# Decoder layer on one core: values' differences in the attention, a later statistic of the recurrence, and three moved pieces of VectorE work

## The chip, the cores and the metric

The kernel runs on one core of one Trainium2 chip. The core has five engines, each of which executes its own list of instructions in order: TensorE (PE in the profile, with its weight loads as PEld), VectorE (DVE), ScalarE (ACT), GpSimd (POOL) and SyncE (SP, which here only issues transfers). They meet through semaphores. The metric is the time of one execution on the device, in microseconds (us); lower is better.

## The reference

One decoder layer over x of shape (1, 512, 1024): a SwiGLU feed-forward half step, a mixer, and a second feed-forward half step, each with an RMS norm ahead of it and one behind it, before the residual is added.

```python
for l in range(DEPTH):                                    # DEPTH = 1
    x = x + 0.5 * rms_norm(swiglu(rms_norm(x, ffn1_pre_g[l]), ffn1_w_gu[l], ffn1_w_down[l]), ffn1_post_g[l])
    y = hybrid_mixer(rms_norm(x, mix_pre_g[l]), ...)
    x = x + rms_norm(y, mix_post_g[l])
    x = x + 0.5 * rms_norm(swiglu(rms_norm(x, ffn2_pre_g[l]), ffn2_w_gu[l], ffn2_w_down[l]), ffn2_post_g[l])
```

The mixer projects its input, runs a gated recurrence (RG-LRU) on 512 channels and attention on the other 512, and projects both back:

```python
y_lru  = rg_lru(x_lru, conv_w, conv_b, w_rg, b_rg, w_ig, b_ig, lam) * gelu(gate_lru)
y_attn = sliding_window_sink_attention(q, k, v, sinks)
y = concatenate([rms_norm(y_lru, g_lru_out), rms_norm(y_attn, g_attn_out)]) @ w_o
```

In the recurrence log_a = 8 · r · log_sigmoid(lam), where lam is a parameter of 512 numbers; its log_sigmoid does not depend on x. The attention has 8 query heads, 2 key/value heads of 64, blocks of 128 queries and a window of 128 keys. A query i of block b sees the keys j ≤ i of its own block and the keys j > i of the block before it, 128 keys in all, and a sink that enters the denominator only:

```python
rel = qi + BLOCK_Q - kj                  # kj runs over the block before and the block itself
band = (rel >= 0) & (rel < WINDOW)
p = exp(scores - m);  denom = sum(p) + exp(sink - m)
out = (p / denom) @ v_band
```

The FFN width is 2816. All inputs are float32.

## The kernel before

**Arithmetic.** Activations are kept transposed: 128 features on the partitions, 512 tokens along the row. A float32 product on TensorE is made of three fast ones: each operand is split into a rounded high part (a cast on ScalarE, tiles `whi_…`, `hha`, `hhs`, `xch`) and the rest (a subtraction, mostly on VectorE, tiles `wlo_…`, `hla`, `hls`, `xcl`), and high·high, high·low and low·high are added up in PSUM (`mm3`, lines 511 to 513). The FFN products use seven products of half-size blocks for eight, so VectorE also makes sums and differences of weight blocks (line 296, 329) and of activations (lines 868 and 880, tiles `s3a`, `s4a`).

**Order.** The kernel writes each engine's order out by hand: instructions stand on each engine in the order in which the program issues them, and nothing is reordered. A class of weight units (`W`) works ahead of TensorE: `W.fill(n)` casts and subtracts units until n more are ready than have been taken, `W.take()` hands one over (and fills ahead itself). There are six pairs of high and low tiles. A unit comes out of one of the raw tiles that SP loads; when the last unit of a raw tile is split, SP issues the load of the next one.

**FFN1** runs over five groups of its width. A group's gate and up products are made by `octo`, which takes pieces of other work to issue beside its products (`beside`, by the product they go with); from the third group on, these are the forms of the group before, for `seven_down`, the down products. In group g = 2 one more piece goes there, `decay_factor` (line 1290): log_sigmoid(lam) and its multiples, 17 small VectorE operations on 128x4 numbers, and one Exp on ScalarE, which needs another activation table than the Silu around it.

**The end of a sublayer** (`boundary`, and the last LATE of the 8 chunks of 128 features): the down products of these chunks are made half of the tokens at a time; VectorE adds each to its partial sum (line 697, `yp_a<-ay`), ScalarE squares it, VectorE adds the square to the sum (lines 710 and 714), TensorE sums over the features (`InvRms.stats`, line 555), ScalarE and VectorE form 1/rms as a diagonal matrix `dg`, and TensorE spreads it over the partitions (`InvRms.spread`, line 569). The loop over the late chunks takes each chunk's weights and calls `W.fill(3)`.

**The mixer.** `in_parts` (line 1548) takes a projection's PSUM bank, scales it by the inverse norm `R` (`scaled`, line 1489, tiles `kT` and `qT`), copies its first 128 columns aside (line 1551, into `home`) and splits the rest. Attention runs in 8 units (block b, key/value head n) with four heads each. For a unit, `scores` makes q·k, the exponentials follow, `turn_p` transposes them to `pt`, ScalarE copies them to `pa`, and GpSimd's `affine_select` sets the masked part to zero. For the first block only the own block's keys count. For b > 0 the rows of the block before and those of the own block share one set of 128 columns, since a query sees complementary parts of them: `pp` keeps the part for the block before and `pa` that for the own. `values` multiplies them with `v`, whose 65th column per head is one, so that the denominator falls out with the output. `v`, the first queries and keys all lie in the tile `home[0]`.

**The output projection of the mixer** (lines 1873 to 1908): five early chunks (EARLY) of 128 output features, four feature blocks `ysp[4..7]` of the attention and four, `ysp[0..3]`, of the recurrence. `wo_attn` makes the attention's part first; meanwhile the recurrence's norm (`lrms`, two halves) is finished: its sum of squares `acc_lru` is added up on VectorE, then come `stats`, `dg_lru`, `spread`, and per block two VectorE multiplications (line 1898), a cast on ScalarE (`ylh`) and a subtraction on VectorE (`yll`). Then the products of `ysp[0]` to `ysp[3]` follow.

Of the kernel before, what the change touches and what calls it, by code (L numbers as in the profile page):

```python
# [15 lines left out]
P = 128  # L16
T = 512
# [105 lines left out]
def tile_layer(ctx: ExitStack, tc: tile.TileContext, out: bass.AP, **ins: bass.AP):  # L123
# [1312 lines left out]
    for g, (f0, f1) in enumerate(GROUPS1):  # L1436
        if g:
            beside = hid.seven_forms_of(before, h_hbm[before], dealt_halves=True) if g > 1 else {}
# [109 lines left out]
    def in_parts(b, first, name, low=dve):  # L1548

        x = scaled(wt(name), b)  # L1550
        dve.tensor_copy(first, x[:, :P])
# [159 lines left out]
    def turn_p(b, n):  # L1711
# [7 lines left out]
        pp = None  # L1719
        if b > 0:  # L1720
            pp = wt(f"pp{b}{n}")
            pool.affine_select(v4(pp), v4(pa), pattern=[[0, NB], [-1, P]], base=0, channel_multiplier=1, compare_op=ALU.is_gt, fill=0.0)
        pool.affine_select(v4(pa), v4(pa), pattern=[[0, NB], [1, P]], base=0, channel_multiplier=-1, compare_op=ALU.is_ge, fill=0.0)
        unit[b, n] = pa, pp

    def values(b, n):
        pc, pp = unit[b, n]
# [5 lines left out]

        for j in range(4):
# [138 lines left out]
    def wo_attn(cs):  # L1873
        ks = range(KC, KD)
        for k in ks:
            for c in cs:
                for part in ws[c]:
                    pe.matmul(banks[c], part[:, k, :], ysp[k][0], start=k == KC and part is ws[c][0], stop=False)
        for c in cs:
            for k in ks:  # L1880
                pe.matmul(banks[c], ws[c][0][:, k, :], ysp[k][1], start=False, stop=False)

    ws, banks = [], []
    for c in range(EARLY):
# [4 lines left out]
        wo_attn(range(c + 1) if c == EARLY - 3 else [c])  # L1889
        if c == EARLY - 3:  # L1890
            for l in lrms:
                l.stats()
            W.fill(3)
        if c == EARLY - 2:
            bcs = [l.spread() for l in lrms]
            for ci in range(KC):
                for h in range(2):
                    dve.tensor_mul(hl[ci][:, HALF[h]], hl[ci][:, HALF[h]], bcs[h])
                y = t2k(f"ylh{ci}", F32R), t2k(f"yll{ci}", F32R)
                x_high(y, hl[ci], col("g_lru_out", ci), ALL)  # L1900
                x_low(y, hl[ci], col("g_lru_out", ci), ALL)
                ysp[ci] = y
# [205 lines left out]
```

## Time and profile before

| | |
|---|---|
| three runs | 840.01, 841.22, 841.30 us (median 841.22) |
| the profiled execution | 840.68 us, its span in the profile 838.7 us |
| TensorE busy | 830.4 us (99% of the span) |
| VectorE busy | 732.4 us (87%) |
| ScalarE busy | 519.2 us (62%) |
| GpSimd busy | 166.8 us (20%) |
| granted TensorE clock | 0.999 |
| DMA | 144.22 MB, mean 172 GB/s |

A row of a timeline gives the start in us from the span's start, the duration in us, the engine, the line of the kernel, the operation, the tile written and those read, the tile's shape, a count, and in brackets how long the engine was idle ahead of it and what ended that. "x2" or "x4" at a row's end means so many like instructions in a row, and the duration is of all. TensorE pipelines its products: the row of a 128x512 product says 0.39 us, but the next one of the same kind starts 0.23 us later. TensorE counts as busy while a product that has started waits within its row, so short waits do not show as idle time; they show when the distance from one start to the next is longer than for the same products elsewhere. The profiled execution takes 1.98 us more than its span.

### The profile page before, as it was taken

The page shows a single profiled execution, that of the slowest core. Times are in us where ns is not written, and L with a number is a line of the kernel's source. Part 1 is how long each engine was busy: PE and PEld are TensorE (multiplying, and loading weights), DVE is VectorE, ACT ScalarE, POOL GpSimd, SP SyncE. Part 2 cuts the span into 40 slices and gives each one's busy share as a digit, 9 for nine tenths or more (in the row PEclk, how much of TensorE's full clock was granted, in tenths as well). Part 3 has the DMA queues.
Part 4 walks back from the last instruction along what each step waited for, and adds up shares of the span by engine and source line. Part 5 has one row for each costly group of instructions (what it writes and reads, how often), then busy time and mean ns, then how long its engine had stood idle before and what let it go on. Part 6 is the DMA issues. An engine that isn't in the chain of part 4 may idle for free.

```text
span 838.7 us, 11907 instructions
## 1 busy us (share of the span) xinstructions
PE 830.4 (99%) x4252; PEld 705.9 (84%) x4252; DVE 732.4 (87%) x1036; ACT 519.2 (62%) x813; POOL 166.8 (20%) x188
## 2 busy tenths in 40 slices
PE   9999999999999999999999999999999999999997
PEld 9988888788888898987788899888888888888885
DVE  4989698999989978889789589997999799898996
ACT  6646556586666654556797446545758667676562
POOL 2022000041320325414531052002004023032001
PEclk9999999999999999999999999999999999999999
DMA  7276407299595797522511131667339939769742
GB/s 252 102 274 227 150 11 263 100 254 301 118 259 188 181 283 228 188 82 88 158 51 51 51 114 39 127 173 252 104 116 243 314 84 255 239 153 260 299 142 101
DMA packets 121851, 144.22 MB, mean 172 GB/s; under 512 B 24184, under 2 KB 76736, under 8 KB 121280
## 3 DMA queue, kind: packets, MB, share of 16 engines
q1 hardware_dynamic: 107824, 112.91, 42.1%
q0 software_dynamic: 13824, 30.42, 16.5%
q8 instruction: 33, 0.54, 0.2%
q14 instruction: 26, 0.21, 0.1%
q10 hardware_dynamic: 144, 0.13, 0.0%
HBM read 100.45 MB, written 39.32 MB: 167 GB/s over the span
## 4 chain that ended last, share of the span: by engine, by line
PE 89%; DVE 6%; DMA 2%; ACT 1%; issue 1%; DVEq 0%; POOL 0%; ACTq 0%; POOLq 0%
PE ab L968 10%; PE aa L968 9%; PE db L968 5%; PE da L968 5%; PE bb L968 3%; PE ba L968 3%; PE ya L1362 3%; PE yaa L1362 2%; PE yda L1362 2%; PE a_first L1230 1%; PE yab L1949 1%; PE yab L1948 1%; PE yab L1947 1%; PE yea L1362 1%; PE mn L529 1%; PE an L529 1%
## 5 line engine op out<-in xcount | busy, mean ns | idle before, releaser
L1140 POOL DMA_DIRECT2D yr_a<-stage x36 | 31.6, 1014 | 177.9 <-ACT stage L1137 157.1
L1140 POOL DMA_DIRECT2D yp_b<-stage x42 | 36.5, 1062 | 147.1 <-ACT stage L1137 117.9
L1963 POOL DMA_DIRECT2D yp_b<-stage x8 | 4.4, 547 | 65.2 <-ACT stage L1962 64.8
L691 POOL TENSOR_TENSOR acca_r<-acca_r,sq_r 128x512 f32<-128x512 f32 x6 | 9.0, 1505 | 40.0 <-ACT sq_r L541 39.9
L529 PE MATMUL an<-xh_mx,whi_xl 128*128 128x256 f32 x64 | 15.9, 288 | 0.0
L530 PE MATMUL an<-xh_mx,wlo_xl 128*128 128x256 f32 x64 | 15.5, 283 | 0.0
L2066 POOL TENSOR_TENSOR last<-yp,grow 128x512 f32<-128x512 f32 x3 | 3.9, 1300 | 56.1 <-DVE yp L2056 56.1
L2063 ACT ACTIVATE ysq<-yp 128x512 f32<-128x512 f32 (+1 forms) x8 | 4.9, 607 | 16.2 <-DVE yp L2056 16.2
L511 PE MATMUL gt<-xh_mx,whi_gt 128*128 128x512 f32 x32 | 14.3, 446 | 0.0
L1399 POOL DMA_DIRECT2D yp_a<-zy x16 | 8.8, 555 | 25.4 <-DMA rows_a<-yr_a 17.2
L511 PE MATMUL pq<-xh_mx,whi_q 128*128 128x512 f32 x32 | 12.8, 400 | 0.0
L511 PE MATMUL pub<-xh_f,whi_bu 128*128 128x512 f32 x32 | 12.7, 395 | 0.0
L513 PE MATMUL gt<-xh_mx,wlo_gt 128*128 128x512 f32 x32 | 12.6, 394 | 0.0
L511 PE MATMUL pgb<-xh_f,whi_bg 128*128 128x512 f32 x32 | 12.6, 393 | 0.0
L512 PE MATMUL gt<-xl_mx,whi_gt 128*128 128x512 f32 x32 | 12.5, 392 | 0.0
L512 PE MATMUL pq<-xl_mx,whi_q 128*128 128x512 f32 x32 | 12.5, 391 | 0.0
L513 PE MATMUL pq<-xh_mx,wlo_q 128*128 128x512 f32 x32 | 12.5, 390 | 0.0
L513 PE MATMUL pgb<-xh_f,wlo_bg 128*128 128x512 f32 x32 | 12.5, 390 | 0.0
L513 PE MATMUL pub<-xh_f,wlo_bu 128*128 128x512 f32 x32 | 12.5, 389 | 0.0
L512 PE MATMUL pgb<-xl_f,whi_bg 128*128 128x512 f32 x32 | 12.5, 389 | 0.0
L512 PE MATMUL pub<-xl_f,whi_bu 128*128 128x512 f32 x32 | 12.5, 389 | 0.0
L1362 PE MATMUL ya<-whi_ad,hha 128*128 128x512 f32 x32 | 12.4, 389 | 0.0
(2018 smaller groups left out, 3415.9 us busy)
## 6 DMA issues: line engine op xcount, KB each, us to landing
yp_b<-stage POOLq DMA_DIRECT2D x50, 256.0 KB, 8.9
yr_a<-stage POOLq DMA_DIRECT2D x44, 256.0 KB, 9.7
h_a<-za SPq DMA_DIRECT2D x16, 256.0 KB
h_b<-zb SPq DMA_DIRECT2D x16, 256.0 KB
hxb<-h_b SPq DMA_DIRECT2D x16, 256.0 KB
hxa<-h_a SPq DMA_DIRECT2D x6, 512.0 KB
xn<-in_x SPq DMA_DIRECT2D x8, 256.0 KB
raw_ad<-in_ffn_w_down SPq DMA_DIRECT2D x2, 1024.0 KB
```

What stands on the lines that cost most here:

```text
L511: pe.matmul(ps, hi[:, k, :], xh, start=start, stop=False)
L512: pe.matmul(ps, hi[:, k, :], xl, start=False, stop=False)
L513: pe.matmul(ps, lo[:, k, :], xh, start=False, stop=stop)
L529: pe.matmul(ps[:, sl], hi[:, k, :], xh, start=k == 0 and not goes_on, stop=False, skip_group_check=True)
L530: pe.matmul(ps[:, sl], lo[:, k, :], xh, start=False, stop=False, skip_group_check=True)
L691: eng.tensor_add(acc, acc, square(part, ALL, f"{self.name}{c}"))
L968: pe.matmul(b[tb], x[:, blk], w[:, k, :], start=first and q + k + j == 0, stop=q + k == 2 and j == 2, skip_group_check=True)
L1140: pool.dma_start(o, st, accum_op=ALU.add)
L1230: pe.matmul(banks[j][:, HALF[0]], ws[j][part][:, k, :], n1.xs[k][xpart][:, HALF[0]], start=k == 0 and part == xpart, stop=stop and k == KD ...
L1362: pe.matmul(o, x[:, blk], a[:, k, :], start=start and j == 0, stop=stop and j == 2, skip_group_check=True)
L1399: (pool if q % 2 else sync).dma_start(chunks[32 * q:32 * (q + 1), :, i * P:(i + 1) * P], turned[32 * i:32 * (i + 1), :, q])
L1947: pe.matmul(banks[i], hh[:, js], hi[:, k, :], start=first and k == 0, stop=False, skip_group_check=True)
```

## The change

It has five parts.

1. `decay_factor` is issued beside the third product of group g = 1 instead of group g = 2.
2. In the loop over FFN1's late chunks `W.fill(3)` becomes `W.fill(2)`.
3. `in_parts` makes the first 128 columns by a multiplication from the PSUM bank, ahead of `scaled`, instead of a copy behind it.
4. The attention's values: for b > 0 the unmasked weights `pa` are multiplied with the block before, and the masked ones (`pc`, the own block's part) with the difference of the two blocks' values. The second `affine_select` of these six units goes. The differences are made by two subtractions, one of 128x325 ahead of the last query chunk's `lru_gates`, and one of 128x65 in the third turn of the attention loop, into the place of the keys that have been used by then.
5. The recurrence's norm: `stats` moves from ahead of the fourth early chunk to the middle of its attention part, `spread` and the four blocks' work from ahead of the fifth chunk to its fourth product, and `W.fill(3)` ahead of them becomes `W.fill(2)` there and `W.fill(1)` behind the loop.

```diff
             beside = hid.seven_forms_of(before, h_hbm[before], dealt_halves=True) if g > 1 else {}
-            if g == 2:
-                beside[2] = [lambda: decay.append(decay_factor())]
...
+            beside = hid.seven_forms_of(before, h_hbm[before], dealt_halves=True) if g > 1 else {2: [lambda: decay.append(decay_factor())]}
...
                 late.append((c, W.take(0)))
-                W.fill(3)
+                W.fill(2)
...
     def in_parts(b, first, name, low=dve):
+        dve.tensor_mul(first, b[:, :P], R[:, :P])
         x = scaled(wt(name), b)
-        dve.tensor_copy(first, x[:, :P])
...
         b = in_product(f"pq{j}")
+        if j == KC - 1:
+            e = HD + 1
+            steps_of_v = [k0[:, :e]] + [home[0][:, P + 2 * T + i * e:P + 2 * T + (i + 1) * e] for i in range(8, 13)]
+            dve.tensor_sub(home[0][:, P + 2 * T + 8 * e:P + 2 * T + 13 * e], v[:, 3 * e:], v[:, e:6 * e])
...
-        pp = None
-        if b > 0:
-            pp = wt(f"pp{b}{n}")
-            pool.affine_select(v4(pp), v4(pa), ..., compare_op=ALU.is_gt, fill=0.0)
-        pool.affine_select(v4(pa), v4(pa), ..., compare_op=ALU.is_ge, fill=0.0)
-        unit[b, n] = pa, pp
+        pc = wt(f"pc{b}{n}") if b > 0 else pa
+        pool.affine_select(v4(pc), v4(pa), ..., compare_op=ALU.is_ge, fill=0.0)
+        unit[b, n] = pa, pc
...
             if b > 0:
-                pe.matmul(o, pp[:, hs], rows(b - 1), start=True, stop=False)
-            pe.matmul(o, pc[:, hs], rows(b), start=b == 0, stop=True)
+                pe.matmul(o, pa[:, hs], rows(b - 1), start=True, stop=False)
+            pe.matmul(o, pc[:, hs], step, start=b == 0, stop=True)
...
+            if now == 2:
+                dve.tensor_sub(steps_of_v[0], v[:, 2 * e:3 * e], v[:, :e])
...
+            for fn in hooks.get(k, ()):
+                fn()
...
-        wo_attn(range(c + 1) if c == EARLY - 3 else [c])
+        wo_attn(range(c + 1) if c == EARLY - 3 else [c],
+                {EARLY - 2: {KD - 1: [l.stats for l in lrms]}, EARLY - 1: {KC + 1: [spread_lru]}}.get(c, {}))
         if c == EARLY - 3:
-            for l in lrms:
-                l.stats()
-            W.fill(3)
-        if c == EARLY - 2:
-            bcs = [l.spread() for l in lrms]
-            ...
+            W.fill(2)
+    W.fill(1)
```

The lines left out behind `spread` are those of the new function `spread_lru`, word for word the same work.

The first place, on VectorE in group 1's `octo`. `wlo_at` and `wlo_au` are low parts of weight units. Before:

```order
L289 TENSOR_TENSOR wlo_at__1054<-raw_ax__667,whi_at__1053 128x1024
L289 TENSOR_TENSOR wlo_at__1073<-raw_ax__741,whi_at__1072 128x1024
L289 TENSOR_TENSOR wlo_au__1092<-raw_ay__882,whi_au__1091 128x1024
L289 TENSOR_TENSOR wlo_au__1113<-raw_ay__885,whi_au__1112 128x1024
L289 TENSOR_TENSOR wlo_av__1129<-raw_ay__882,whi_av__1128 128x1024
```

And now:

```order
L289 TENSOR_TENSOR wlo_at__1054<-raw_ax__667,whi_at__1053 128x1024
L1298 TENSOR_SCALAR nabs<-cols 128x4
L1299 TENSOR_TENSOR nabs<-nabs,cols 128x4
L1303 TENSOR_SCALAR s<-z 128x4
L1304 RECIPROCAL s<-s 128x4
L1305 TENSOR_TENSOR s<-s,z 128x4
L1307 TENSOR_TENSOR s_1100<-s 128x4
L1309 TENSOR_SCALAR q<-s_1100 128x4
L1311 SCALAR_TENSOR_TENSOR q<-q,s_1100 128x4 x6
L1312 SCALAR_TENSOR_TENSOR q<-q,s 128x4
L1315 TENSOR_SCALAR ka<-cols 128x4
```

Two more rows (lines 1316 and 1318) follow, then `wlo_at__1073`. The whole of `decay_factor` has moved ahead of it, from its old place in group 2's `octo` between two rows `wlo_at`; ScalarE's table load and Exp move with it.

The second place, on VectorE at the end of FFN1. `wlo_xl` are low parts of weights of the mixer's projection, `yp_a` partial sums, `accb_r` the sum of squares. Before:

```order
L215 TENSOR_TENSOR wlo_xl_1_3219<-raw_xl__3090,whi_xl_1_3218 128x1024
L215 TENSOR_TENSOR wlo_xl_0_3248<-raw_xl__3189,whi_xl_0_3247 128x1024
L697 TENSOR_TENSOR yp_a_3135<-ay_3268,yp_a_3135 128x256
L710 TENSOR_TENSOR accb_r_3070<-acca_r_3069,sq_r_3288 128x256
L697 TENSOR_TENSOR yp_a_3135<-ay_3291,yp_a_3135 128x256
L714 TENSOR_TENSOR accb_r_3070<-accb_r_3070,sq_r_3311 128x256
L697 TENSOR_TENSOR yp_a_3135<-ay_3314,yp_a_3135 128x256
```

And now:

```order
L215 TENSOR_TENSOR wlo_xl_1_3219<-raw_xl__3090,whi_xl_1_3218 128x1024
L697 TENSOR_TENSOR yp_a_3135<-ay_3264,yp_a_3135 128x256
L710 TENSOR_TENSOR accb_r_3070<-acca_r_3069,sq_r_3284 128x256
L697 TENSOR_TENSOR yp_a_3135<-ay_3287,yp_a_3135 128x256
L714 TENSOR_TENSOR accb_r_3070<-accb_r_3070,sq_r_3307 128x256
L215 TENSOR_TENSOR wlo_xl_0_3311<-raw_xl__3189,whi_xl_0_3310 128x1024
L697 TENSOR_TENSOR yp_a_3135<-ay_3314,yp_a_3135 128x256
```

The unit of `raw_xl__3189` now comes behind two of the late chunks' sums instead of ahead of all four.

The third place, on TensorE in the mixer's output projection: the fourth and fifth early chunks. Before, both `stats` stand ahead of the fourth chunk's 12 products and both `spread` ahead of the fifth chunk's 12; these are the rows around `spread`:

```order
L1881 MATMUL wo_4749<-yal_4643,whi_wo_1_4498 128x512
L569 MATMUL rms_lru_4721<-dg_lru_4728,ones 128x256
L569 MATMUL rms_lru_4730<-dg_lru_4737,ones 128x256
L1878 MATMUL wo_4788<-attn,whi_wo_0_4739 128x512
L1878 MATMUL wo_4788<-attn,wlo_wo_0_4740 128x512
```

And now, from `stats`:

```order
L555 MATMUL rms_lru_4730<-mean_c,acc_lru 128x1 x2
L555 MATMUL rms_lru_4739<-mean_c,acc_lru 128x1 x2
L1886 MATMUL wo_4721<-attn,whi_wo_1_4496 128x512
L1886 MATMUL wo_4721<-yal_4631,whi_wo_1_4496 128x512
L1886 MATMUL wo_4721<-yal_4635,whi_wo_1_4496 128x512
L1886 MATMUL wo_4721<-yal_4639,whi_wo_1_4496 128x512
L1881 MATMUL wo_4752<-attn,whi_wo_0_4717 128x512
L1881 MATMUL wo_4752<-attn,wlo_wo_0_4718 128x512
L1881 MATMUL wo_4752<-yah_4630,whi_wo_0_4717 128x512
L1881 MATMUL wo_4752<-yah_4630,wlo_wo_0_4718 128x512
L569 MATMUL rms_lru_4730<-dg_lru_4737,ones 128x256
L569 MATMUL rms_lru_4739<-dg_lru_4746,ones 128x256
```

`stats` comes 8 products later, `spread` 4 products later; between the two stand 8 products instead of 12, and between `spread` and the first product of the recurrence's `ylh` 8 instead of 12. On VectorE the low part of the sixth chunk's weights, which stood between `dg_lru` and the multiplications by the spread norm, now stands behind the last `yll`; the load of the raw tile that it frees is issued that much later.

More of the change, by code (lines that the diff above doesn't have):

```diff
@@ L1718, in turn_p @@
         act.copy(pa, pt)
-        pp = None
-        if b > 0:
-            pp = wt(f"pp{b}{n}")
-            pool.affine_select(v4(pp), v4(pa), pattern=[[0, NB], [-1, P]], base=0, channel_multiplier=1, compare_op=ALU.is_gt, fill=0.0)
-        pool.affine_select(v4(pa), v4(pa), pattern=[[0, NB], [1, P]], base=0, channel_multiplier=-1, compare_op=ALU.is_ge, fill=0.0)
-        unit[b, n] = pa, pp
+        pc = wt(f"pc{b}{n}") if b > 0 else pa
+        pool.affine_select(v4(pc), v4(pa), pattern=[[0, NB], [1, P]], base=0, channel_multiplier=-1, compare_op=ALU.is_ge, fill=0.0)
+        unit[b, n] = pa, pc
     def values(b, n):
-        pc, pp = unit[b, n]
+        pa, pc = unit[b, n]
         po = bank(f"po{b}{n}")[:, :4 * (HD + 1)]
@@ L1732, in rows @@
             return v[:, (2 * b + n) * (HD + 1):(2 * b + n + 1) * (HD + 1)]
+        step = steps_of_v[2 * b - 2 + n] if b > 0 else rows(b)
         for j in range(4):
@@ L1871, in tile_layer, with wo_attn @@
     EARLY = KD - LATE
-    def wo_attn(cs):
+    def wo_attn(cs, hooks={}):
         ks = range(KC, KD)
@@ L1881, in wo_attn, with spread_lru @@
                 pe.matmul(banks[c], ws[c][0][:, k, :], ysp[k][1], start=False, stop=False)
+    def spread_lru():
+        bcs = [l.spread() for l in lrms]
+        for ci in range(KC):
+            for h in range(2):
+                dve.tensor_mul(hl[ci][:, HALF[h]], hl[ci][:, HALF[h]], bcs[h])
+            y = t2k(f"ylh{ci}", F32R), t2k(f"yll{ci}", F32R)
+            x_high(y, hl[ci], col("g_lru_out", ci), ALL)
+            x_low(y, hl[ci], col("g_lru_out", ci), ALL)
+            ysp[ci] = y
     ws, banks = [], []
@@ L1888, in tile_layer @@
             continue
-        wo_attn(range(c + 1) if c == EARLY - 3 else [c])
+        wo_attn(range(c + 1) if c == EARLY - 3 else [c],
+                {EARLY - 2: {KD - 1: [l.stats for l in lrms]}, EARLY - 1: {KC + 1: [spread_lru]}}.get(c, {}))
         if c == EARLY - 3:
-            for l in lrms:
-                l.stats()
-            W.fill(3)
-        if c == EARLY - 2:
-            bcs = [l.spread() for l in lrms]
[L1896 to L1902, printed above, removed]
+            W.fill(2)
+    W.fill(1)
     for k in (0, 1):
```

1 line of the change is left out of this document (removed).

## The prediction

> **What bounds the kernel now.** I read the page's busy times first, then what TensorE waits for, then the timelines around each place that the change touches.
>
> ```profile
> PE 830.4 (99%) x4252; PEld 705.9 (84%) x4252; DVE 732.4 (87%) x1036; ACT 519.2 (62%) x813; POOL 166.8 (20%) x188
> PE rms_lru L555 <- DVE acc_lru L1863: 0.3, 1, 0.3
> ```
>
> TensorE is the bound: 99% busy. The number of its products doesn't change, so only its waits can be gained or lost. One of 0.3 us stands under its own name; shorter ones hide inside busy rows, and are found by the distance of the starts. The rest of the prediction is a list of such places. The bound of what counts: 0.2% is 1.7 us, about what a measurement of this kernel can tell from no change (the three runs lie 1.29 us apart).
>
> **Part 1, `decay_factor` leaves group 2.** The down products of group 1, on TensorE:
>
> ```profile
> 165.39 0.39 PE L1362 MATMUL yaa<-whi_ads__1565,hls 128*128 128x512 f32 x1
> 165.81 0.50 PE L1362 MATMUL yea<-whi_adt__1592,hhs 128*128 128x512 f32 x1
> 166.29 0.49 PE L1362 MATMUL yea<-wlo_adt__1593,hhs 128*128 128x512 f32 x1
> 166.89 0.50 PE L1362 MATMUL yea<-whi_adt__1592,hls 128*128 128x512 f32 x1
> 167.23 0.39 PE L1362 MATMUL yea<-whi_adt__1592,hhs 128*128 128x512 f32 x1
> 169.76 0.50 PE L1362 MATMUL yda<-whi_adu__1642,hla 128*128 128x512 f32 x1
> 170.10 0.40 PE L1362 MATMUL yda<-whi_adu__1642,hha 128*128 128x512 f32 x1
> ```
>
> Undisturbed, such products start 0.23 us apart (165.39 to 165.62 would be next). Four distances, 165.39 to 167.23, take 1.84 instead of 0.91 us, the one at 169.76 takes 0.34 instead of 0.23: 0.93 + 0.11 = 1.04 us are lost. VectorE and ScalarE, there and some 33 us earlier:
>
> ```profile
> 133.07 0.16 DVE L1298 TENSOR_SCALAR nabs<-cols 128x4 f32<-128x4 f32 x1
> 136.45 1.22 DVE L289 TENSOR_TENSOR wlo_at__1366<-raw_ax__1095,whi_at__1365 128x1024 fp32r<-128x1024 f32 x1
> 166.16 0.68 DVE L851 TENSOR_TENSOR hls<-s4a,hhs 128x512 fp32r<-128x512 f32 x1
> 169.03 0.68 DVE L851 TENSOR_TENSOR hla<-hxa,hha 128x512 fp32r<-128x512 f32 x1
> 129.30 1.28 ACT L1301 ACT_TABLE_LOAD   x1
> 133.47 0.21 ACT L1301 ACTIVATE z<-nabs 128x4 f32<-128x4 f32 x1 [2.88 <-DVE nabs L1299]
> 142.77 1.28 ACT L995 ACT_TABLE_LOAD   x1
> 144.06 1.09 ACT L995 ACTIVATE p1a<-ba 128x512 f32<-128x512 f32 x2
> ```
>
> `hls` ends at 166.84 and TensorE's product with it starts at 166.89; `hla` ends at 169.71 and its product starts at 169.76. So VectorE is late there, by the whole 1.04 us for `hla`, which without the four waits would have been wanted 0.93 us earlier still. `decay_factor` holds VectorE for 136.45 − 133.07 = 3.38 us, and ScalarE for a table load, a wait of 2.88 us and a second load, back to Silu's table. From there to 166 us VectorE hardly stands still, so what is taken away at 133 arrives at 166 nearly whole: 3.4 us against the 1.04 that were missing. The stall goes, all 1.04 us. The lower end is 0.5, half of it, if the cast `hhs` or another step behind VectorE is late next.
>
> The new place must take it:
>
> ```profile
> 91.23 1.23 DVE L289 TENSOR_TENSOR wlo_at__1073<-raw_ax__741,whi_at__1072 128x1024 fp32r<-128x1024 f32 x1 [1.22 <-ACT whi_at__1072 L285]
> 96.67 1.23 DVE L289 TENSOR_TENSOR wlo_au__1113<-raw_ay__885,whi_au__1112 128x1024 fp32r<-128x1024 f32 x1 [2.16 <-ACT whi_au__1112 L285]
> 101.44 1.22 DVE L289 TENSOR_TENSOR wlo_av__1145<-raw_ay__885,whi_av__1144 128x1024 fp32r<-128x1024 f32 x1 [1.50 <-ACT whi_av__1144 L285]
> 104.12 1.23 DVE L289 TENSOR_TENSOR wlo_ap__1166<-raw_ax__1076,whi_ap__1165 128x1024 fp32r<-128x1024 f32 x1 [1.46 <-ACT whi_ap__1165 L285]
> ```
>
> These four waits alone are 6.34 us within 14 us, so 3.4 us of small operations and some wait for Exp fit. In order: `wlo_at__1073` could start at 91.2, when its cast is done; behind that cast ScalarE loads the table (1.28) and takes the Exp (0.21), VectorE finishes the block (from 133.68 to 136.45: 2.77), so it starts at 95.5. The SP queue's next load, which waits for it, slips by the same 4 us. The way back to Silu's table falls on ScalarE, 1.28 us, some 10 us later. I cost the new place at nothing; its cover is these waits, and without them it costs up to 3.4 + 2 × 1.28 = 5.9 us.
>
> Here a rule speaks against the change. The Trainium skill, "ScalarE: Activation LUTs", section "What ACT_TABLE_LOAD costs", puts a drain of some 1.38 us on top of each load. The trace differs: `p1a` starts 0.01 us behind the load's 1.28. By the page the two loads would cost ScalarE an estimated 2.8 us more, part of which would meet the casts of the next units; by the row, nothing more, and the sum goes by the row.
>
> **Part 2, one unit later at FFN1's end.**
>
> ```profile
> 333.32 1.05 ACT L210 CAST whi_xl<-raw_xl__3189 128x1024 fp32r<-128x1024 f32 x1 [2.03 <-DMA raw_xl__3189<-in_w_in]
> 334.40 1.23 DVE L215 TENSOR_TENSOR wlo_xl<-raw_xl__3189,whi_xl 128x1024 fp32r<-128x1024 f32 x1 [2.20 <-ACT whi_xl L210]
> 340.90 0.42 DVE L565 TENSOR_TENSOR dg_r<-ident,rs_r 128x256 f32<-128x256 f32 x1
> 339.33 0.28 PE L513 MATMUL ay<-hha,wlo_ad 128*128 128x256 f32 x1
> 342.10 0.28 PE L512 MATMUL ay<-hla,whi_ad 128*128 128x256 f32 x1
> 496.61 0.28 PE L513 MATMUL my<-ylh,wlo_wo 128*128 128x256 f32 x1
> 499.16 0.28 PE L512 MATMUL my<-yll,whi_wo 128*128 128x256 f32 x1
> ```
>
> VectorE stands in front of a weight that hasn't landed (2.20 us), and the late chunks' sums queue behind it up to `dg_r`, which TensorE's spread needs. What TensorE loses is read against the mixer's own boundary, the same stretch from the last product ahead of `stats` to the second behind `spread`. There it takes 2.55 us with 12 products between the two, here 2.77 with 9; three products of 0.12 less would be 2.19, so 0.58 us are lost. With the unit moved behind two sums, the first sums start up to 2.2 us earlier, and the unit, landed by then, costs VectorE its 1.1 us in the chain's own gaps. But the last chunk's sum and the root before `dg_r` keep their own pace, so I take 0.40 of 0.58 (lower end 0.1, upper 0.58).
>
> **Part 3 and 4, first columns and values.**
>
> ```profile
> 403.06 1.14 DVE L1551 COPY home<-qT 128x128 f32<-128x128 f32 x1
> 407.08 0.23 DVE L1551 COPY home<-qT 128x128 f32<-128x128 f32 x1
> 406.36 0.69 DVE L1489 TENSOR_TENSOR qT<-pq,R_mx 128x512 f32<-128x512 f32 x1 [0.43 <-PE pq L513]
> 404.74 2.34 POOL L1524 TENSOR_TENSOR xc<-ig,xc 128x512 f32<-128x512 f32 x1 [0.63 <-DMA ig<-other]
> 407.06 1.05 PE L1661 MATMUL cur<-home 64*128 64x128 f32 x16
> ```
>
> The five copies, 0.23 to 1.14 us, become multiplications from PSUM; of 128x128 they can't exceed `qT`'s 0.69 us for four times the columns, and I take 0.3. TensorE waits for none but the last, and that comes earlier (ahead of `qT`, not behind). Zero on the path. Six `affine_select` go from GpSimd, which is 20% busy; TensorE's eight products per unit stay, and none waits for GpSimd in the list of waits: zero.
>
> New are the two subtractions. The large one (325 of 512 columns: 0.69 × 325 / 512 = 0.44 us) stands ahead of the last query chunk, in VectorE's gap of 0.43 us before 406.36. Against it speaks GpSimd's row: 2.34 us, until 407.08, and the small copy started exactly then, while `qT`, which reads PSUM, took its 0.69 us beside it. By these rows the subtraction may be held up to 407.08 and end at 407.5; the last queries' multiplication follows, to 407.8, and TensorE's scores of the first block, 16 from 407.06 on in 1.05 us, come to the last four of these queries at 407.06 + 0.75 = 407.8. I take a loss of 0.10 (lower end 0, upper 0.5). The small subtraction (128x65) goes where VectorE waits: zero. The Trainium skill, "SBUF — State Buffer", section "SBUF: two separate sides", says that a VectorE operation with two SBUF inputs and a GpSimd operation exclude each other for the whole instruction; the trace agrees in that a copy took 1.14 us where another took 0.23. Were the subtraction beside it free, as `qT` is, the loss would be 0.
>
> **Part 5, the recurrence's statistics.**
>
> ```profile
> 461.65 0.84 PE L1881 MATMUL wo<-yal,whi_wo 128*128 128x512 f32 x3
> 462.78 1.05 PE L555 MATMUL rms_lru<-mean_c,acc_lru 128*128 128x1 f32 x8 [0.29 <-DVE acc_lru L1863]
> 466.55 1.02 PE L569 MATMUL rms_lru<-dg_lru,ones 128*128 128x256 f32 x4
> 470.18 0.39 PE L511 MATMUL wo<-ylh,whi_wo 128*128 128x512 f32 x1
> 464.58 0.42 DVE L565 TENSOR_TENSOR dg_lru<-ident,rs_lru 128x256 f32<-128x256 f32 x1
> 467.38 0.74 DVE L1898 TENSOR_TENSOR xc<-xc,rms_lru 128x256 f32<-128x256 f32 x2
> 468.92 0.75 DVE L588 SCALAR_TENSOR_TENSOR yll<-xc,cols,ylh 128x512 fp32r<-128x512 f32 x1 [0.79 <-ACT ylh L585]
> ```
>
> The three products before `stats` need 0.68, so it could start at 462.33; it starts at 462.78. Behind eight more products that wait of 0.45 us goes, less a hand-over: 0.40. `dg_lru` is done 465.00 − 462.78 = 2.22 us after `stats` starts, and `spread` will then be 0.9 for `stats` and 8 × 0.23 behind: 2.7. It holds. But behind `spread` the cover shrinks: 470.18 − 466.55 = 3.63 us to the first product of `ylh`, less four products, 2.72, and the second product, which reads `yll`, at 2.95. From `spread`'s start to `yll`'s end it is at most 468.92 + 0.75 − 466.55 = 3.12 us: late by 0.17 or less. So a new wait of 0.15 (0 to 0.2), and 0.25 net (0.1 to 0.45). The later three blocks come 2.2 us apart while each serves 15 products of 0.23, 3.4 us: covered. The low part that stands behind the last `yll` now delays a load of SP by some 10 us, which later chunks use; zero if it lands, and TensorE's list of waits has no transfer in it.
>
> **The sum.** 1.04 + 0.40 − 0.10 + 0.25 = 1.59 us gained against the profiled execution's 840.68 us (838.7 in the span, 1.98 around it, unchanged): 839.1. That execution lies 0.54 below the median of the three runs, 841.22; the mean of the four times is 840.80, and from it 839.2 follows, which I forecast: 0.24% under the median shown.
>
> **The rivals.**
> - Part of it only: the stall at 165 us is filled by whatever is late behind VectorE (the cast `hhs`, or a form's transfer), or the boundary's last sum sets `dg_r` as before. For it speaks that every place here is a matter of tenths; against it the 3.4 us that meet a lack of 1.04. With half of part 1 and the low ends of the others (0.5 + 0.1 − 0.1 + 0.1 = 0.6): 840.2.
> - Slower, by part 1's new place: ScalarE's second table load falls at 101 us, where its casts and VectorE's low parts of the next units wait for one another. If VectorE comes to 107 us late by more than the 3.4 − 1.04 = 2.3 us that are to spare, the stall at 165 stays in part, and from 3.4 on it is longer than before; at the full 5.9 us it is 5.9 − 3.4 = 2.5 us longer, and with the other parts' gain of 0.55: 840.8 + 2.5 − 0.55 = 842.7, or more where a load that slipped lands late. The 6.34 us of waits speak against it.
> - The change doesn't do what it says: the lateness at 165 us is not VectorE's queue but something that keeps its own time, and the other gains cancel: 840.8.
>
> **Chances.** The forecast's case, 838.3 to 839.9, 0.62; part of it only, 840.0 to 840.6, 0.22; slower by the new place, 842.7 or above, 0.10; nothing, 0.06. The low end takes all upper ends, 1.04 + 0.58 + 0.45 = 2.07, from the lowest run, 840.01: 838.0. The high end takes in the second case and most of the fourth: 841.0. Against the median, faster by over 0.2% (under 839.54) is the forecast's case without its upper part and a little luck of the others: 0.63; within 0.2%: 0.27; slower: 0.10.
>
> **What would show it.** In the profile after: starts 0.23 us apart from 165 to 170 us, and VectorE done with `hls` ahead of its product; small 128x4 rows at 90 to 96 us with TensorE undisturbed to 120; no wait of 2.2 us ahead of `wlo_xl`, and `spread` following its products without a gap; `stats` of the recurrence gone from the list of waits, and at most 0.2 us ahead of the first `yll` product. Wrong would be: a gap on TensorE between 100 and 125, `cur` (first-block scores) waiting at 407, `yll` late by more than 0.5, or a transfer that takes TensorE's time after 480.

## The result and the profile after

Over 20 executions of each kernel the median went from 840.68 to 839.38 us; the ratio is 0.9985, with a 95% interval of 0.9979 to 0.9991. That is 1.3 us faster, 0.15%: a gain that can be told from nothing, but less than the 0.2% (1.7 us) that the prediction set as its bound. The forecast of 839.2 us and its range, 838.0 to 841.0, held the time. That range is 3 us wide and holds the 840.68 us of the kernel before as well, so by itself it tests little. Of the three chances against the median, "faster by over 0.2%" (0.63) did not come true, and "within 0.2%" (0.27) did. The median of three runs shown before, 841.22, lay 0.54 us above that of the 20.

The profiled execution of the changed kernel took 840.0 us, with a span of 838.2. First the page's busy times and the whole of TensorE's list of waits:

```profile
PE 830.1 (99%) x4252; PEld 706.0 (84%) x4252; DVE 731.1 (87%) x1038; ACT 520.3 (62%) x813; POOL 162.1 (19%) x182
PE warm L1217 <- POOL ident masks.py:199: 1.4, 1, 1.4
PE xtp L1164 <- DMA xn<-in_x: 0.2, 1, 0.2
```

The recurrence's `rms_lru` is gone from the list; what stands there now is at the program's start, where the input lands. That start differs from one execution to the next and hides part of the gain in this one. So I compare stretches: the distance between the starts of the same two TensorE products, in the profiles of both kernels.

| stretch on TensorE | before, us | after, us | difference |
|---|---|---|---|
| program's start, to the 191st product | 26.97 | 27.81 | +0.84 |
| `decay_factor`'s new place (88 to 125 us) | 36.95 | 36.95 | 0 |
| its old effect: last `yaa` to second `yda` behind `hla` | 4.71 | 3.63 | −1.08 |
| FFN1's boundary: last product ahead of `stats` to the second behind `spread` | 2.77 | 2.35 | −0.42 |
| last query product to the first gate product behind the first block's scores | 2.10 | 2.52 | +0.42 |
| attention, from there to 455 us | 47.04 | 47.07 | +0.03 |
| recurrence's norm: first `yal` product ahead of it to the third product of `ylh` | 8.99 | 8.68 | −0.31 |
| from there to the last product | 361.51 | 361.54 | +0.03 |

The stretches between these differ by 0.03 us or less. Without the program's start, the parts sum to −1.08 − 0.42 + 0.42 − 0.31 = −1.39 us, near the measured −1.3.

The rows of the timeline that answer to those of the prediction. TensorE and VectorE at the old place's effect:

```profile
166.24 0.39 PE L1362 MATMUL yaa<-whi_ads__1565,hls 128*128 128x512 f32 x1
166.46 0.39 PE L1362 MATMUL yea<-whi_adt__1592,hhs 128*128 128x512 f32 x1
166.69 0.39 PE L1362 MATMUL yea<-wlo_adt__1593,hhs 128*128 128x512 f32 x1
166.92 0.39 PE L1362 MATMUL yea<-whi_adt__1592,hls 128*128 128x512 f32 x1
169.86 0.39 PE L1362 MATMUL yda<-whi_adu__1642,hha 128*128 128x512 f32 x1
163.23 0.68 DVE L851 TENSOR_TENSOR hls<-s4a,hhs 128x512 fp32r<-128x512 f32 x1
```

All starts are 0.23 us apart. `hls` is done at 163.91, 3.0 us ahead of its product; before, it was done 0.05 us ahead of a product that had waited. The new place, VectorE and ScalarE:

```profile
93.59 0.17 DVE L1303 TENSOR_SCALAR s<-z 128x4 f32<-128x4 f32 x1 [2.44 <-ACT z L1301]
96.33 1.22 DVE L289 TENSOR_TENSOR wlo_at__1073<-raw_ax__741,whi_at__1072 128x1024 fp32r<-128x1024 f32 x1
105.62 1.23 DVE L289 TENSOR_TENSOR wlo_ap__1191<-raw_ax__1076,whi_ap__1190 128x1024 fp32r<-128x1024 f32 x1 [2.11 <-ACT whi_ap__1190 L285]
92.05 1.28 ACT L1301 ACT_TABLE_LOAD   x1
102.28 1.28 ACT L995 ACT_TABLE_LOAD   x1
103.57 1.09 ACT L995 ACTIVATE p1a<-ba 128x512 f32<-128x512 f32 x2
```

VectorE stands 2.44 us in front of the Exp and still waits for ScalarE again at 105.62: the room was there. `wlo_at__1073` starts at 96.33, which is the 95.5 worked out, 0.8 us later as all of this execution. `p1a` starts 0.01 us behind the end of the load, as before. FFN1's boundary:

```profile
335.89 1.23 DVE L215 TENSOR_TENSOR wlo_xl<-raw_xl__3189,whi_xl 128x1024 fp32r<-128x1024 f32 x1 [0.51 <-ACT whi_xl L210]
340.22 0.42 DVE L565 TENSOR_TENSOR dg_r<-ident,rs_r 128x256 f32<-128x256 f32 x1
339.06 0.28 PE L513 MATMUL ay<-hha,wlo_ad 128*128 128x256 f32 x1
341.41 0.28 PE L512 MATMUL ay<-hla,whi_ad 128*128 128x256 f32 x1
```

The wait of 2.20 us ahead of `wlo_xl` has become 0.51, and the unit fits between the sums. The first block's scores, with VectorE, GpSimd and TensorE:

```profile
404.38 1.21 DVE L215 TENSOR_TENSOR wlo_gt<-raw_gt__3800,whi_gt 128x1024 fp32r<-128x1024 f32 x1
405.52 1.58 DVE L1571 TENSOR_TENSOR home<-home 128x325 f32<-128x325 f32 x1
407.01 0.28 DVE L1548 TENSOR_TENSOR home<-pq,R_mx 128x128 f32<-128x128 f32 x1
404.58 2.15 POOL L1522 TENSOR_TENSOR xc<-ig,xc 128x512 f32<-128x512 f32 x1 [0.68 <-DMA ig<-other]
405.25 0.39 PE L513 MATMUL pq<-xh_mx,wlo_q 128*128 128x512 f32 x1
406.37 1.47 PE L1663 MATMUL cur<-home 64*128 64x128 f32 x16
407.77 0.50 PE L511 MATMUL gt<-xh_mx,whi_gt 128*128 128x512 f32 x1
```

The large subtraction takes 1.58 us, more than three times its estimate of 0.44: GpSimd's multiplication, which began at 404.58 and ends at 406.73, is served first, and the subtraction ends 0.36 us behind it. The last queries' columns are done at 407.29, and `cur` takes 1.47 us instead of 1.05. Last, the recurrence's norm:

```profile
463.90 0.95 PE L555 MATMUL rms_lru<-mean_c,acc_lru 128*128 128x1 f32 x8
466.66 1.03 PE L569 MATMUL rms_lru<-dg_lru,ones 128*128 128x256 f32 x4
469.37 0.40 PE L511 MATMUL wo<-ylh,whi_wo 128*128 128x512 f32 x1
469.75 0.50 PE L512 MATMUL wo<-yll,whi_wo 128*128 128x512 f32 x1
470.08 0.39 PE L513 MATMUL wo<-ylh,wlo_wo 128*128 128x512 f32 x1
468.94 0.75 DVE L588 SCALAR_TENSOR_TENSOR yll<-xc,cols,ylh 128x512 fp32r<-128x512 f32 x1 [0.79 <-ACT ylh L585]
```

`stats` no longer waits. But `yll` ends at 469.69, and the products around it start 0.38 and 0.33 us apart: 0.25 us over two times 0.23 come back.

### The profile page after: what moved, and what is told of

Same layout as the page of the kernel before. It is cut to its first block, busy times and chain, and to the rows that moved or that the text cites. A ratio compares the mean times of both kernels' runs of the same rounds, so it can differ in the third digit from the quotient of the medians.

```text
span 838.2 us, 11891 instructions
## 1 busy us (share of the span) xinstructions
PE 830.1 (99%) x4252; PEld 706.0 (84%) x4252; DVE 731.1 (87%) x1038; ACT 520.3 (62%) x813; POOL 162.1 (19%) x182
## 4 chain that ended last, share of the span: by engine, by line
PE 94%; DVE 2%; DMA 1%; ACT 1%; issue 1%; SPq 0%; POOL 0%; DVEq 0%; POOLq 0%
PE ab L968 10%; PE aa L968 10%; PE db L968 5%; PE da L968 5%; PE yaa L1362 3%; PE bb L968 3%; PE ba L968 3%; PE ya L1362 3%; PE yda L1362 2%; PE aa L898 1%; PE a_first L1230 1%; PE yab L1954 1%; PE yab L1955 1%; PE yab L1953 1%; PE wo L1881 1%; DVE xc L1507 1%
```

## The experiments

Every run below was profiled once; the two at the end were also timed over several executions. The stretches are those of the table, all in us. One profile can differ from another where nothing was edited: in six of these (parts 1, 2, 3, and 3 and 4 alone, the subtraction later, the norm earlier) TensorE lost another 0.3 to 0.5 us at some 314 us, and in that of part 2 alone another 0.4 us at 443 us.

| kernel | start | old effect of `decay_factor` | boundary | scores | norm |
|---|---|---|---|---|---|
| before | 26.97 | 4.71 | 2.77 | 2.10 | 8.99 |
| part 1 alone | 26.89 | 3.63 | 2.51 | 2.49 | 9.00 |
| part 2 alone | 27.11 | 4.71 | 2.35 | 2.10 | 8.98 |
| part 3 alone | 26.91 | 4.72 | 2.48 | 2.10 | 8.95 |
| parts 3 and 4 alone | 27.35 | 4.71 | 2.63 | 2.55 | 8.97 |
| part 5 alone | 27.47 | 4.71 | 2.35 | 2.10 | 8.67 |
| all parts (first profile) | 27.81 | 3.63 | 2.35 | 2.52 | 8.68 |
| all parts (again) | 27.05 | 3.63 | 2.35 | 2.52 | 8.67 |
| all, subtraction in two | 26.81 | 3.63 | 2.35 | 2.31 | 8.67 |
| all, subtraction later | 27.47 | 3.63 | 2.35 | 2.10 | 8.67 |
| all, norm earlier | 27.42 | 3.63 | 2.35 | 2.52 | 8.43 |
| all, both edits | 27.11 | 3.63 | 2.35 | 2.10 | 8.43 |

### Part 1 alone

```diff
-            if g == 2:
-                beside[2] = [lambda: decay.append(decay_factor())]
+            beside = ... if g > 1 else {2: [lambda: decay.append(decay_factor())]}
```

> The kernel before with the first part alone: decay_factor in group 1. Theory (VectorE's queue is what makes TensorE wait at 165 us): from the last product yaa ahead of yea to the second yda behind hla, 4.71 us before, 3.67 us now (1.04 less), and nothing changes at 90 to 120 us or behind 170 us. Rival (something else is late there, and the parts of the change behind it brought the gain): 4.7 us as before.

The stretch is 3.63 us, 1.08 less, and the products from 88 to 125 us take 36.95 us, as before. The theory holds: part 1 needs no other part for this gain. But the scores at 406 us, which the part doesn't touch, took 2.49 instead of 2.10. VectorE, then GpSimd, in this run:

```profile
403.64 2.34 DVE L215 TENSOR_TENSOR wlo_gt<-raw_gt__3800,whi_gt 128x1024 fp32r<-128x1024 f32 x1
403.62 1.28 POOL L1522 TENSOR_TENSOR xc<-ig,xc 128x512 f32<-128x512 f32 x1 [0.59 <-DMA ig<-other]
```

And VectorE at the same place of the kernel before, whose GpSimd row (404.74, 2.34 us) stands in the prediction:

```profile
404.72 1.21 DVE L215 TENSOR_TENSOR wlo_gt<-raw_gt__3800,whi_gt 128x1024 fp32r<-128x1024 f32 x1
```

There VectorE began 0.02 us ahead of GpSimd, took 1.21 us, and GpSimd's multiplication was stretched to 2.34. Here GpSimd began 0.02 us ahead, took its 1.28, and VectorE's subtraction was stretched to 2.34. It ended 1.1 us later against TensorE's products, the last queries' columns came 0.6 us later, and TensorE lost 0.39 us. The one that starts first goes through, the other pays. Which one it is was decided by 0.02 us; in the profiles of part 2 and of part 5 alone VectorE is ahead by less than that.

### Part 2 alone

```diff
                 late.append((c, W.take(0)))
-                W.fill(3)
+                W.fill(2)
```

> The kernel before with the second part alone: one unit fewer ahead in the loop over FFN1's late chunks. Theory (the sums queued behind a weight that hasn't landed): the stretch at the boundary from the last product ahead of stats to the second behind spread, 2.77 us before, shrinks to 2.35 us, as with the whole change. Rival (it needs the lead of part 1): 2.6 us or more.

2.35 us, so it doesn't need part 1. But the kernels without part 2 took 2.77, 2.51, 2.48, 2.63 and 2.35 in their five profiles. The stretch follows the time that VectorE stands in front of the unit of `raw_xl__3189`: 2.20, 1.85, 1.85, 1.99 and 1.54 us. In the last of these, with part 5 alone, ScalarE's wait for the transfer was shorter than the 2.03 us of the profile before:

```profile
332.69 1.05 ACT L210 CAST whi_xl<-raw_xl__3189 128x1024 fp32r<-128x1024 f32 x1 [0.93 <-DMA raw_xl__3189<-in_w_in]
```

What the part gains depends on when the transfer lands in that execution: from 0 to 0.42 us, 0.20 in the mean of the five. With the part, the stretch is 2.35 in every run.

### Parts 3 and 4

Part 3 alone is the line in `in_parts`; parts 3 and 4 together are that and the attention's values.

> The kernel before with part 3 alone, the first columns by a multiplication from PSUM. Theory: rows of 0.28 us in place of 0.23 to 1.14, nothing gained or lost on TensorE (under 0.05 us in the stretch from the last pq product to the first gt product, 2.11 us). Rival: some of the loss at 407 us is its doing, 0.1 us or more.

> The kernel before with parts 3 and 4 alone. Theory: from the last pq product ahead of the gates to the first gt product behind the first block's scores, 2.11 us before, it takes about 2.5 us: the large subtraction waits for GpSimd and with it the last queries. All else is unchanged, so this kernel is some 0.4 us slower than before. Rival (only together with the lead of the other parts does it collide): 2.1 us.

Part 3 alone: 2.10 us at the scores, its five multiplications 0.28 or 0.29 us each. With part 4: 2.55 us. So the loss of 0.4 us comes with part 4, and it doesn't need the lead of the others.

But part 3 is not without effect there: it moves GpSimd's multiplication. Against the start of the last query product, that row begins 1.20 us earlier in the kernel before, and 1.22 with part 1 alone, although TensorE is 1.1 us ahead by then. It begins 0.73 us earlier with part 3 alone, 0.64 with parts 3 and 4, 0.67 in the changed kernel. TensorE's last query product and GpSimd, with part 3 alone:

```profile
405.97 0.39 PE L513 MATMUL pq<-xh_mx,wlo_q 128*128 128x512 f32 x1
405.24 2.23 POOL L1524 TENSOR_TENSOR xc<-ig,xc 128x512 f32<-128x512 f32 x1 [0.61 <-DMA ig<-other]
```

In all of these it begins 2.8 or 2.9 us behind the end of ScalarE's `other`, whose transfer it waits for, and `other` ends 4.02 us ahead of the last query product without part 3 and some 3.5 with it. The multiplications that part 3 puts ahead of the scaled query chunks push these back, the second one (`qT`) by 0.48 us; the cast behind it, and what follows on ScalarE, come as much later. Part 3 alone loses nothing by this; part 4's subtraction has to wait for that row. Part 4 was not run without part 3, so how the loss divides between the two is not shown.

Two runs on the cause of the loss, both with the changed kernel. First the large subtraction in two:

```diff
-            dve.tensor_sub(home[0][:, P + 2 * T + 8 * e:P + 2 * T + 13 * e], v[:, 3 * e:], v[:, e:6 * e])
+            dve.tensor_sub(home[0][:, P + 2 * T + 8 * e:P + 2 * T + 10 * e], v[:, 3 * e:5 * e], v[:, e:3 * e])
...
             if now == 2:
                 dve.tensor_sub(steps_of_v[0], v[:, 2 * e:3 * e], v[:, :e])
+                dve.tensor_sub(home[0][:, P + 2 * T + 10 * e:P + 2 * T + 13 * e], v[:, 5 * e:], v[:, 3 * e:6 * e])
```

> The changed kernel with the large subtraction in two: 128x130 in its place, 128x195 in the third turn of the attention loop. Theory (it is held by GpSimd's multiplication, which was waiting first): the smaller one's row is still 1.2 to 1.4 us long, since only its own 0.26 us fewer are saved, and TensorE's scores still wait, by 0.15 us instead of 0.41. Rival (it is slow by its size, 1.58 us for 325 columns): 0.63 us, and no wait.

VectorE and GpSimd of this run:

```profile
404.50 1.37 DVE L1571 TENSOR_TENSOR home<-home 128x130 f32<-128x130 f32 x1
403.57 2.15 POOL L1522 TENSOR_TENSOR xc<-ig,xc 128x512 f32<-128x512 f32 x1 [0.69 <-DMA ig<-other]
```

With 40% of the columns it still takes 1.37 us: GpSimd ends at 405.72, the subtraction 0.15 us later. It is held, not slow. TensorE's wait falls to 2.31 − 2.10 = 0.21 us. Then the subtraction wholly in the third turn, its place ahead of the last queries left empty:

```diff
-            dve.tensor_sub(home[0][:, P + 2 * T + 8 * e:P + 2 * T + 13 * e], v[:, 3 * e:], v[:, e:6 * e])
...
             if now == 2:
                 dve.tensor_sub(steps_of_v[0], v[:, 2 * e:3 * e], v[:, :e])
+                dve.tensor_sub(home[0][:, P + 2 * T + 8 * e:P + 2 * T + 13 * e], v[:, 3 * e:], v[:, e:6 * e])
```

> The changed kernel with the large subtraction wholly in the third turn of the attention loop, where VectorE waits for ScalarE. Theory: from the last pq product to the first gt product 2.1 us as before the change (2.52 with it), the subtraction's row 0.5 us, nothing new behind it: 0.4 us faster than the changed kernel. Rival (another piece holds the last queries, their multiplication from PSUM): 2.5 us.

VectorE of this run, and GpSimd at the scores:

```profile
404.35 1.21 DVE L215 TENSOR_TENSOR wlo_gt<-raw_gt__3800,whi_gt 128x1024 fp32r<-128x1024 f32 x1
405.61 0.29 DVE L1548 TENSOR_TENSOR home<-pq,R_mx 128x128 f32<-128x128 f32 x1
414.98 0.49 DVE L1780 TENSOR_TENSOR home<-home 128x325 f32<-128x325 f32 x1
416.22 1.23 DVE L215 TENSOR_TENSOR wlo_wo<-raw_wo__3907,whi_wo 128x1024 fp32r<-128x1024 f32 x1 [0.75 <-ACT whi_wo L210]
404.51 2.20 POOL L1522 TENSOR_TENSOR xc<-ig,xc 128x512 f32<-128x512 f32 x1 [0.64 <-DMA ig<-other]
```

The scores are back at 2.10 us, the subtraction takes 0.49 where VectorE still waits 0.75 us behind it. The multiplication from PSUM takes 0.29 us in the middle of GpSimd's row. And `wlo_gt` now starts 0.16 us ahead of GpSimd, not 0.02: in the kernels with part 3 that distance is 0.13 to 0.23 us, so the toss-up is gone there. Behind it there is a small loss. In the three kernels with some or all of the large subtraction in the third turn, TensorE loses 0.10 us at some 504 us (a product `mn` ahead of the second feed-forward step), and in none of the nine other kernels of the table; the cause stays open.

### Part 5 alone

The edit is that of `wo_attn`, `spread_lru` and the fills.

> The kernel before with part 5 alone. Theory: the wait of 0.45 us ahead of stats goes, and up to 0.2 us comes back behind the first ylh product and none elsewhere: net 0.25 to 0.3 us. Rival (without part 1 to 4 the load that starts 10 us later or the casts collide): a wait of TensorE behind 470 us that the kernel before doesn't have.

8.67 us, 0.32 less; the stretch behind it, to the end, takes 361.56 against 361.51. The load that starts later costs nothing.

### The norm two products earlier

```diff
-                {EARLY - 2: {KD - 1: [l.stats for l in lrms]}, EARLY - 1: {KC + 1: [spread_lru]}}.get(c, {}))
+                {EARLY - 2: {KD - 2: [l.stats for l in lrms]}, EARLY - 1: {KC: [spread_lru]}}.get(c, {}))
```

> The changed kernel with the recurrence's stats and its spread each two products earlier. Theory (what is left there is the chain from spread to yll, 0.2 us too long for eight products): with ten products behind spread the distance of the first ylh and the first yll product falls from 0.38 to 0.23 us and the next from 0.33 to 0.23, and stats and spread still don't wait: 0.25 us faster. Rival: spread now waits for dg_lru, by 0.2 us or more.

8.43 us, 0.24 less than with the change as it is. The chain from `spread` to `yll` was what was left.

### Both edits, and the change again

> The changed kernel with the large subtraction in the third turn and with stats and spread two products earlier. From TensorE's starts 0.41 + 0.25 = 0.66 us less than the changed kernel, so some 1.9 us less than the kernel before (0.9977).

> The changed kernel again, beside the one with both edits: 1.2 to 1.3 us faster than before (0.9985), and TensorE's starts as in its first profile, apart from the transfers at the program's start.

Timed in the same five rounds: the kernel before 841.08 us, the change again 839.52 (ratio 0.9982, 0.9973 to 0.9991), both edits 838.73 (0.9972, 0.9962 to 0.9982). The stretches give 0.42 + 0.24 = 0.66 us between the last two, and 0.56 with the 0.10 us lost at 504 us; the medians give 0.79. The intervals of the two ratios overlap, so that the step is shown by the stretches rather than by the times. TensorE of the kernel with both edits:

```profile
468.20 0.39 PE L511 MATMUL wo<-ylh,whi_wo 128*128 128x512 f32 x1
468.43 0.39 PE L512 MATMUL wo<-yll,whi_wo 128*128 128x512 f32 x1
468.65 0.39 PE L513 MATMUL wo<-ylh,wlo_wo 128*128 128x512 f32 x1
```

### VectorE's time or ScalarE's table loads at the old place

Two kernels add idle work at the old place of `decay_factor`: the first its 17 VectorE operations without the Exp, in new tiles of 128x4; the second only the Exp, with its two table loads, in one new tile.

```diff
+            if g == 2:
+                beside[2] = [filler]
```

> The changed kernel with the 17 small VectorE operations of decay_factor made once more, to no use, at their old place in group 2, without the Exp and the table loads. Theory (VectorE's time is what counted): about 3.2 us of VectorE bring the stall at 165 us back, 0.8 to 1.04 us. Rival (the two table loads and ScalarE's wait counted): no stall.

> The changed kernel with one Exp of 128x4 at its old place in group 2, to no use, and so with both table loads there, but without VectorE's operations. Theory (VectorE's time is what counted): no stall at 165 us, 0 to 0.1 us. Rival (ScalarE's table loads, 2.56 us, delay the casts that VectorE waits for): a stall of 0.5 us or more.

With VectorE's 17 operations, from 134.37 to 137.52, the stretch at 165 us is 3.70 us, 0.07 more than without: nearly no stall, against 0.8 to 1.04 expected. With the Exp alone it is 3.63. VectorE and TensorE there, of the kernel with the filler and then of that with the Exp:

```profile
166.43 0.69 DVE L851 TENSOR_TENSOR hls<-s4a,hhs 128x512 fp32r<-128x512 f32 x1
167.37 0.40 PE L1385 MATMUL yea<-whi_adt__1614,hls 128*128 128x512 f32 x1
```

```profile
165.41 0.70 DVE L851 TENSOR_TENSOR hls<-s4a,hhs 128x512 fp32r<-128x512 f32 x1
167.37 0.39 PE L1366 MATMUL yea<-whi_adt__1594,hls 128*128 128x512 f32 x1
```

`hls` is done 0.25 and 1.26 us ahead of its product; in the changed kernel 3.0. So VectorE has lost 2.75 us of lead with the filler and 1.7 with the Exp. Up to 133 us both engines are 0.46 us later than in the changed kernel, VectorE as much as TensorE, so what is lost is lost from there on.

With the filler VectorE falls 3.15 us behind, takes up 0.4 of it where it would have waited, and keeps the rest until `hls`. With the Exp alone it falls behind in two steps: 0.92 us at 136.65, where `hla` waits for the cast below, and 0.79 at 145.89, where the same of the next block waits behind the load of Silu's table.

```profile
136.00 0.62 ACT L843 CAST hha<-hxa 128x512 fp32r<-128x512 f32 x1 [2.96 <-DMA hxa<-h_a]
142.03 1.28 ACT L995 ACT_TABLE_LOAD   x1
145.89 0.69 DVE L851 TENSOR_TENSOR hla<-hxa,hha 128x512 fp32r<-128x512 f32 x1 [0.70 <-ACT hha L843]
```

The first step is not the Exp's: in the kernel with the filler, which has no Exp there, the transfer of `hxa` is as late (that cast starts at 136.03; in the changed kernel at 134.61). The second is. In the kernel before both came together: of VectorE's 3.38 us 2.97 were left at 142 us, and 0.79 were added at the same `hla`, 3.76 in all against the 3.0 that were to spare. That VectorE's operations alone make the stall is refuted: they use up the lead, and the load of Silu's table makes them late.

Both kernels are far slower for another reason: 851.04 and 844.63 us in one execution each, against 840.98 for the kernel before beside them. TensorE loses time in places that have nothing to do with the edit, first at 23 us (its stretch of the program's start is 28.27 and 28.29 us, against 26.81 to 27.81 in the twelve others), then, by the changed kernel's clock, at 285, 313 to 315 and 804 us, where it waits for ScalarE and VectorE. Ahead of 313 us VectorE had stood 4.3 and 4.1 us in front of a transfer (`rows_a`), against 0.7 to 1.6 us in the others. From the list of TensorE's waits of the kernel with the Exp:

```profile
PE ya L511 <- ACT hha L905: 1.1, 1, 1.1
PE a_first L529 <- ACT xh_a L585: 0.7, 1, 0.7
```

The hardware queue's packets take 43.0% and 42.6% of 16 engines' span in these two, against 41.9% to 42.2% in the others. The same bytes take more time. Up to 23 us both make the same instructions as the others; what may differ is where buffers lie, since the new 16-byte tiles of the `const` pool can move what is laid out behind them. That moved buffers slow the transfers is my reading; it was not tried by itself, and it stays open.

## Why the prediction was right, and where it wasn't

- **What bounds the kernel.** TensorE, at 99%, and only its waits counted: right. Between the two profiles each of the prediction's places showed up in the stretches, and beside the program's start no other did.
- **Part 1**, 1.04 us gained, nothing lost at the new place: 1.08 and 0.00. The rule of the Trainium skill on the table load ("ScalarE: Activation LUTs", "What ACT_TABLE_LOAD costs"), a drain of some 1.38 us on top, is not borne out: both loads at the new place are followed within 0.02 us. One argument under it was too narrow: that VectorE's 3.38 us were what counted. Of these 2.97 arrived, and ScalarE's second table load added 0.79: before, `hls` was done at 166.84 for a product that could have started at 165.39 + 3 × 0.23 = 166.08, 0.8 us late; now it is 3.0 us early.
- **Part 2**, 0.40 us taken: 0.42 in the profile, but this term was mis-sized all the same. It was read from one execution in which the transfer landed late. Over five profiles without the part it is 0.20.
- **Parts 3 and 4.** The multiplications at 0.3 us and at nothing on the path: 0.28 us, and alone nothing. The loss from the subtraction was seen, with its place and its mechanism, but taken as 0.10 (0 to 0.5) and measured 0.42. The step that failed is the arithmetic "held up to 407.08 and end at 407.5", multiplication "to 407.8". It took GpSimd's row to end where it did before, 1.15 us behind the start of the last query product (407.08 − 405.93). In the changed kernel it ends 1.48 us behind (406.73 − 405.25), and 1.5 also with parts 3 and 4 alone, so the gains upstream are not the reason: with part 1 alone, 1.1 us ahead, GpSimd's row moved with TensorE. Part 3 moves it: it makes ScalarE's `other` 0.5 us late, and the transfer that GpSimd waits for with it. The prediction asked what part 3's rows do to TensorE, not what they do to the row that part 4 waits for. The last queries' columns came 2.04 us behind that product (407.29 − 405.25), not 1.87 (407.8 − 405.93); TensorE's last four `cur` began 0.31 us late, and it lost another 0.1 behind them. One sign it read was none: the copy that "started exactly then", at 407.08, stands behind `qT`, which ended at 407.05; with part 1 alone it starts as soon behind `qT`, and GpSimd's multiplication had ended 1.7 us before. And the copy of 1.14 us, read as a sign of the two engines' exclusion, has one SBUF input; the subtractions of 2.34 and 1.58 us are the rows with two.
- **Part 5**, 0.40 less 0.15, net 0.25: 0.31. `yll` came back with 0.25 us, not 0.15 (0 to 0.2), and 0.31 + 0.25 = 0.56 us were gained where 0.40 were taken.
- **The sum.** 1.59 us were forecast; the stretches gave 1.39 in the profile, and with part 2 at its mean 1.17. The rest of the distance to the bound of 0.2% is the starting point: against 840.68, the median of 20, the forecast time of 839.2 is 0.18% less. The forecast time lies 0.18 us from the measured median although the gain was 0.29 us short (1.30 against 1.59): the start it was taken from, 840.80, lay 0.12 us above the median of 20. That the two times lie so near is luck in part. The forecast's case was right in its mechanism but for parts 3 and 4, and the chance of 0.63 for "over 0.2%" was too high for a sum that lay on the bound.
- **The rivals.** "Part of it only" said 840.2: the stall at 165 us was not refilled. "Slower by the new place" would have needed VectorE to come to 107 us late by more than 2.3 us: at its second `u4a` there it is as far from TensorE as before (both some 0.85 us later than in the profile before), and TensorE lost nothing by 125 us. "The change doesn't do what it says" falls with part 1 alone, which takes the stall at 165 us away.

## What to carry to other kernels

A stall on a full engine is measured by the distance between two fixed products, in several profiles, not by idle time in one: a stretch that no edit touched read 2.35 to 2.77 us over five profiles, and the program's start 26.81 to 27.81. When an operation is put ahead of another, follow what stands behind it on the other engines too: small multiplications ahead of the scaled chunks made a cast, an activation, a transfer and a GpSimd row 0.5 us late, and the loss came out at an operation that had to wait for that row. And an operation of VectorE with both inputs in SBUF is placed where GpSimd is quiet, or fed from PSUM.

## What the runs showed of the hardware

- A VectorE subtraction (two SBUF inputs) and a GpSimd multiplication did not run side by side: the one that began 0.02 us earlier took 1.21 or 1.28 us, the other 2.34, in both directions. "SBUF — State Buffer" in the Trainium skill, section "SBUF: two separate sides", describes this as an exclusive lock held for the whole instruction, and the rows agree; the multiplication from PSUM was not held (0.29 us in the middle of GpSimd's row).
- Two kernels with new tiles of 16 bytes per partition and a few small instructions more were 3.7 and 10 us slower than the kernel before, in one execution each, with waits far from the added work. The cause is open.
